# The experts' weights in one host array: three pieces of 2 MB an expert, one 16 KB run a partition, one transfer a piece

## The chip, the cores and the metric

The kernel runs on one core of a Trainium2 chip. The metric is the time of the program on the device in microseconds; lower is better. Three runs of the kernel before took 1817.59, 1819.29 and 1819.63 us, with a median of 1819.29 us.

## The reference

One sequence of 256 tokens with 1024 features goes through three blocks, all in float32. The first two (sparse attention beside Mamba2, a short convolution, each followed by a dense feed-forward) and the attention mixer of the third are not touched. The last part is a mixture of 64 experts in 8 groups. Each token takes two experts; the result is added to the residual, and a last norm follows. For one expert and the tokens `xb` routed to it:

```
def expert_block(args):
    xb, e = args
    return (jax.nn.silu(xb @ w1[e]) * (xb @ w3[e])) @ w2[e]
```

`w1[e]` and `w3[e]` are 1024 x 512 and `w2[e]` is 512 x 1024, so each matrix is 2 MB and one expert has 6 MB. All 64 experts together have 384 MB (402.7 million bytes), and each is read once.

## The kernel before

The dense blocks run first: weights come in chunks of 512 KB, are split into two parts for the float32 products, and are multiplied. `Net.experts` (its lines are in the listing) then goes through the 64 experts in order. For each it needs three *pieces* of 2 MB, which lie in SBUF as tiles of 128 partitions x 4096 floats. There are 11 such tiles, the slots (`NSLOT`), reused in turn: piece `i` goes to slot `i % 11`. Pieces 0 and 1 of an expert hold the first and the second half of the rows of w1 and of w3, and piece 2 holds w2.

`Net.slot` issues the transfers of one piece on SP's queue:

- pieces 0 and 1 are two transfers each (line 1100), one from w1 and one from w3. Each is 1 MB; a partition's share is one run of 8 KB (4 rows of 512 floats) in DRAM.
- piece 2 is one transfer of 2 MB (line 1105). A partition's share is four rows of w2, each a run of 4 KB.
- piece 2 of the last expert alone is four transfers of 512 KB (line 1108), one for each block of 256 output columns; a partition's share of one is four runs of 1 KB. The last product can then begin with the first three blocks.

So an expert takes five issues. The loop over experts goes: every fourth expert, the rows of the tokens of four experts are gathered (`gather`, line 1267); `up` multiplies by w1 and w3 (line 1361); `activate` makes silu(gate) * up (lines 1302 to 1310); `down` multiplies by w2 (line 1420); `spread` and `combine` add the result to the residual in PSUM (lines 1318 and 1329). Then `slot` is called for the three pieces that take the slots just used, `i + 11`.

After the 32nd expert `further` handles experts with more than 32 tokens, one round of 32 at a time. It begins with a branch on the number of such rounds (line 1430) that every engine takes, SP too. Its own loads (tile `mw`) are not among the transfers of the profiled execution. `finish` is the last expert's second product, the last norm and the stores.

The two halves of `slot` before:

```
if w < 2:
    for k, n in enumerate(("w1", "w3")):
        src = self.d[n][e].rearrange("(p j) n -> p (j n)", j=8)
        self.nc.sync.dma_start(t[:, k * 2048:k * 2048 + 2048], src[:, w * 2048:w * 2048 + 2048])
else:
    src = self.d["w2"][e].rearrange("(c p) n -> p c n", p=P)
```

Of the kernel before, what the change touches and what calls it, by code (L numbers as in the profile page):

```python
# [17 lines left out]
PSUM = bass.MemoryType.PSUM  # L18

P = 128  # L20
T = 256
# [61 lines left out]
class Turn:  # L83
    """x^T times the gain of the coming norm, split, [128, 8, 256], and the sums of squares of x. head() begins
    what follows with the first block of tokens."""
# [30 lines left out]
class FinalTurn(Turn):  # L116
    """The turn at the first stack's last norm: x times that norm's gain, and the sums of its squares in ss2."""
# [12 lines left out]
class Routing:  # L130
    """At the last norm: the rows for the experts and the logits."""
# [3 lines left out]
    def head(self):  # L135
        pass
# [45 lines left out]
    def rows(self, b, cols):  # L182
        """columns of a block of tokens, split exactly into three bfloat16 parts: the first of them and the rest."""
        net, nc = self.net, self.net.nc
        c0, c1 = cols
        x = net.x[:, b, c0:c1].rearrange("p (q j) -> p j q", j=8)
        if b:
            rest = self.xT[0][:, c0 // P:c1 // P].rearrange("p k t -> p (k t)")
        else:
            rest = net.xt.tile([P, 512], F32, tag="xg", name="rest", bufs=2)  # L190
        rest = self.rest[b, cols] = rest.rearrange("p (j q) -> p j q", j=8)
        g = net.xg[b][0][:, :, c0 // 8:c1 // 8]
        nc.scalar.activation(g, x, AF.Copy)
        nc.vector.tensor_tensor(rest, x, g, op=ALU.subtract)
# [8 lines left out]
class Net:  # L203
# [44 lines left out]
    def btype(self, srcs, xh, xl, first=None, ps=None):  # L248
        """[128 channels, 2 tiles, 256 tokens] of two chunks of 128 output channels (all of K)."""
        ps = self.acc() if ps is None else ps  # L250
        for m in range(2):
            hi, lo = first[m] if first else self.chunk(srcs[m])
            h3, l3 = (t.rearrange("p (k n) -> p k n", k=KT) for t in (hi, lo))
            for k in range(KT):
                self.mm3(ps[:, m * 256:m * 256 + 256], h3[:, k], l3[:, k], xh[:, k], xl[:, k], k == 0, k == KT - 1)
        return ps.rearrange("p (m t) -> p m t", m=2)

    def rstd_of(self, pool, x, n, width, name):
        """rstd[128, n] from sums of squares [128, n]."""
# [6 lines left out]
    def row_of(self, cols, dst):  # L266
        """dst[128, n*128] = the columns cols[128, n], each as a row along the free axis, on every partition."""
# [7 lines left out]
    def out_chunk(self, src, accs, yh, yl, kt, first):  # L275
        """accs[b][half] += y[kt] @ rows of the chunk."""
# [15 lines left out]
    def out_last(self, srcs, ys, accs, first, turn, scale=None, loaded=None):  # L292
        """The last chunks of a projection onto the residual, one block of tokens after the other and for each some
        columns after the others, so that what follows begins with what is done."""
# [36 lines left out]
    def flip(self, b, ks):  # L331
        """PSUM with x^T of some tiles of features of a block of tokens."""
# [5 lines left out]
    def parts16(self, pool, ps, mask, n, name):  # L338
        """ps[3 n rows, 256], the same n rows three times: row i n + h becomes the i-th bfloat16 part of row h."""
# [115 lines left out]
    def layer0(self, turn):  # L455
        tc, nc, d = self.tc, self.nc, self.d
        with ExitStack() as ctx:
# [51 lines left out]
            with tc.tile_pool(name="dsa", bufs=1) as dp:  # L509
                # ckv, iw, dt (token major) and ik (channel major, twice)  # L510
# [113 lines left out]
    def steps(self, op, dtr, dt, a, eb):  # L624
        """dt = softplus(dtr), a = -dt exp(A_log); eb: minus the running sums of a in each chunk, and what is
        left of chunk 0 after each of its tokens."""
# [25 lines left out]
    def mamba_in(self, xh, xl, rb2, xs, zs, bc, cb, eb):  # L652
# [19 lines left out]
        def cbt(g):  # L672
            """C B^T, transposed: [s, l] of (chunk 0, 0), (chunk 0, 1), (chunk 1, 1)."""
# [12 lines left out]
        def decays(q):  # L686
            """exp of the sums of a from s to l, times C B^T, transposed: [s, head, l]."""
# [17 lines left out]
    def mamba(self, ctx, xs, zs, cb, dt, decays, yah, yal, turn):  # L705
# [4 lines left out]
        # x dt, token major  # L710
# [63 lines left out]
    def log1p_exp_neg_abs(self, pool, out, x, t):  # L774
        """out = log(1 + exp(-|x|)) = 2 atanh(e / (2 + e))."""
# [31 lines left out]
    def ffn(self, turn, w, nxt):  # L807
        """The first 256 hidden channels come token major (they begin with the first block of tokens alone), the others
        channel major. The up branch stays without the norm's factor, which the residual applies."""
# [101 lines left out]
    def angles(self, pool):  # L911
        """cos and sin of position * frequency, [128, 2, 32], with the angle taken to [-pi, pi] first."""
# [23 lines left out]
    def atype(self, srcs, n, xh, xl):  # L936
        """[128 tokens, n] of each block of tokens."""
# [11 lines left out]
    def mixer(self, turn):  # L949
        tc, nc, d = self.tc, self.nc, self.d  # L950
        gates_pool = tc.tile_pool(name="b2", bufs=1)
        with gates_pool as gp:
# [3 lines left out]
            with tc.tile_pool(name="att2", bufs=1) as ap:  # L956
# [20 lines left out]
                # 8 log sigmoid  # L977
# [53 lines left out]
                def bias(ps, b, h):  # L1031
                    """minus 8 times the running sum of log f at s, for every t: what is left of the sum over
                    s < k <= t is the same for all s."""
# [56 lines left out]
    def slot(self, i, t=None):  # L1090
        """DMA of piece i of the experts' weights (of expert 0, then of expert 1, ...): rows 8 p + j of w1 and of w3
        for j < 4, for the other j, w2."""
# [4 lines left out]
        if w < 2:  # L1097
            for k, n in enumerate(("w1", "w3")):
                src = self.d[n][e].rearrange("(p j) n -> p (j n)", j=8)
                self.nc.sync.dma_start(t[:, k * 2048:k * 2048 + 2048], src[:, w * 2048:w * 2048 + 2048])  # L1100
        else:
            src = self.d["w2"][e].rearrange("(c p) n -> p c n", p=P)
            dst = t.rearrange("p (c n) -> p c n", c=4)
            if e < NE - 1:
                self.nc.sync.dma_start(dst, src)  # L1105
            else:
                for c in range(4):
                    self.nc.sync.dma_start(dst[:, c].rearrange("p (k n) -> p k n", k=4), src[:, :, 256 * c:256 * c + 256])  # L1108
# [19 lines left out]
    def open_slots(self, name, ids, now=True):  # L1128
        """slots, from the lowest address to the highest in the order of ids."""
# [9 lines left out]
    def take(self, pool, v, top, name):  # L1139
        """v[128, 2, 8] with the first place of each value of top[128, 2, 8] set to TAKEN."""  # L1140
# [5 lines left out]
    def route(self, rp, lg):  # L1146
        """From the logits of groups and experts: the place of every token within its two experts, from 1 on."""
# [39 lines left out]
    def gates(self, rp):  # L1187
        """The gate of every token at its experts, and the rounds of 32 tokens past the first: expert e has more[e]
        of them, the rounds of all experts in one row."""
# [10 lines left out]
        # the first of the two: the first place of the largest  # L1200
# [57 lines left out]
    def gather(self, dest, sel, n):  # L1258
        """dest[128, 8, n] = rows times the gain, feature 8p + j at [p, j], of the tokens that sel[128, 2, n] picks."""
# [13 lines left out]
    def split_rstd(self, pool, rstd):  # L1273
        """the factors of the last norm, split exactly into three bfloat16 parts."""
# [8 lines left out]
    def factors(self, sel, n):  # L1283
        """[32 c + slot, n experts]: the norm's factor of the token in each slot of sel, four times."""
# [11 lines left out]
    def activate(self, pool, ps, rs):  # L1296
        """ps[32 c + slot, 256]: gate features 256 c + f for c < 2, up features 256 (c - 2) + f after them, both
        without the norm's factor rs.
        Returns silu(gate) * up as [128 f, half, c, slot]."""
# [13 lines left out]
    def spread(self, pool, dg):  # L1313
        """the gates dg[128 tokens, 2, 32 c + slot] as [32 c + slot, 256 tokens]."""
# [8 lines left out]
    def combine(self, y, dT, cs=range(4), last=False, busy=0):  # L1323
        """adds y[32 c + slot, 256] to columns 256 c of the tokens."""
# [9 lines left out]
    def sel(self, e, n):  # L1334
        """sel[128 tokens, 2, 32 slots of expert e, of expert e + 1, ...]: which token each slot takes."""
# [75 lines left out]
    def busy(self, rhs, n, lhs=None):  # L1411
        """n products that nobody reads: the array's clock stays up while the last weights arrive."""
# [5 lines left out]
    def down(self, ps, h, w2, k, c, o=None):  # L1418
        o = k * 1024 + c * 256 if o is None else o
# [3 lines left out]
    def further(self, mp):  # L1423
        """Experts with more than 32 tokens: one round of 32 more at a time."""
# [5 lines left out]
        with tc.If(n > 0), tc.For_i(0, n, 1):  # L1430
# [25 lines left out]
            for j in range(8):  # L1456
                for i in range(2):
                    w = mp.tile([P, 512], F32, tag="mw", name="mw")
                    src = d[("w1", "w3")[i]][bass.ds(r, 1)].rearrange("e (p j) n -> p (e j n)", j=8)
                    nc.sync.dma_start(w, src[:, j * 512:j * 512 + 512])  # L1460
# [5 lines left out]
            for k in range(4):  # L1466
                src = d["w2"][bass.ds(r, 1)].rearrange("e (c p) n -> p (e c) n", p=P)
                for i in range(2):
                    w = mp.tile([P, 512], F32, tag="mw", name="mw")
                    nc.sync.dma_start(w, src[:, k, i * 512:i * 512 + 512])  # L1470
# [9 lines left out]
    def finish(self, mp, h, w2, dg, fn):  # L1480
        """The last expert's second product, a block of 256 columns after the other; self.res[c][token, 256 b:][:256]
        is then the residual sum: its norm, and out."""
# [9 lines left out]
        def down(c0, c1):  # L1492
            ps = self.wk()
            for k in range(4):
                for c in range(c0, c1):
                    self.down(ps, h, w2, k, c, c * 1024 + k * 256)
# [107 lines left out]
def layouts(i):  # L1604
# [63 lines left out]
    d["w1"], d["w3"], d["w2"] = i["w1_2"][0], i["w3_2"][0], i["w2_2"][0]  # L1668
# [17 lines left out]
```

## Time and profile before

| | before |
|---|---|
| median of 3 runs | 1819.29 us (1817.59 to 1819.63) |
| span of the profiled execution, first to last instruction | 1817.2 us |
| TensorE busy (share of the span) | 1536.6 us (85%) |
| VectorE, ScalarE busy | 687.9 us (38%), 525.5 us (29%) |
| mean granted TensorE clock | 0.939 of full speed |
| read from HBM | 542.34 MB |

The span is that of one profiled execution. The page gives no other time for this execution; the median of the runs is 2.1 us above its span. Times in the rows below are microseconds from the start of the span, unless marked ns. "Busy" TensorE includes pipelined matmuls, so it is not TensorE at its peak. The share of the 16 DMA engines can be above 1, since the packets of one engine overlap a little in the record.

### The profile page before, as it was taken

The page shows a single profiled execution, that of the slowest core. Times are in us where ns is not written, and L with a number is a line of the kernel's source. Part 1 is how long each engine was busy: PE and PEld are TensorE (multiplying, and loading weights), DVE is VectorE, ACT ScalarE, POOL GpSimd, SP SyncE. Part 2 cuts the span into 40 slices and gives each one's busy share as a digit, 9 for nine tenths or more (in the row PEclk, how much of TensorE's full clock was granted, in tenths as well). Part 3 has the DMA queues.
Part 4 walks back from the last instruction along what each step waited for, and adds up shares of the span by engine and source line. Part 5 has one row for each costly group of instructions (what it writes and reads, how often), then busy time and mean ns, then how long its engine had stood idle before and what let it go on. Part 6 is the DMA issues. An engine that isn't in the chain of part 4 may idle for free. (4 is left out here: it accounts for less than half of the span.)

```text
span 1817.2 us, 34068 instructions
## 1 busy us (share of the span) xinstructions
PE 1536.6 (85%) x14763; PEld 1136.6 (63%) x14763; DVE 687.9 (38%) x1327; ACT 525.5 (29%) x903; POOL 12.7 (1%) x16
## 2 busy tenths in 40 slices
PE   8999999999999999999886677677676767776676
PEld 7988899989899988798553333333343433433333
DVE  6887755577655567457410111011011101110111
ACT  5585544444544455555200000000000000000001
POOL 0000000000000000000000000000000000000000
PEclk9999999999999999999998988888888998888989
DMA  8344876555555523376999999999999999999997
GB/s 295 102 137 139 287 282 185 186 164 185 194 180 186 187 88 117 109 275 217 382 415 415 416 417 415 416 416 416 416 398 371 416 415 416 416 415 415 416 416 277
DMA packets 112856, 545.64 MB, mean 300 GB/s; under 512 B 10048, under 2 KB 12480, under 8 KB 79936
## 3 DMA queue, kind: packets, MB, share of 16 engines
q1 hardware_dynamic: 112704, 543.43, 77.9%
q8 instruction: 118, 1.93, 0.4%
q14 instruction: 34, 0.28, 0.0%
HBM read 542.34 MB, written 1.05 MB: 299 GB/s over the span
## 5 line engine op out<-in xcount | busy, mean ns | idle before, releaser
L1361 PE MATMUL wk<-w,xe 128*32 128x256 f32 x4096 | 322.2, 410 | 103.0 <-DMA w<-in_w 98.2
L233 DVE TENSOR_TENSOR wlo<-raw,whi 128x1024 fp32r<-128x1024 f32 (+1 forms) x208 | 252.6, 1219 | 152.2 <-ACT whi L232 150.8
L1361 PEld LDWEIGHTS wk<-w,xe 128*32 128x32 f32 x4096 | 146.8, 115 | 249.2 <-DMA w<-in_w 142.3
L232 ACT ACTIVATE whi<-raw 128x1024 fp32r<-128x1024 f32 (+1 forms) x208 | 217.8, 1055 | 251.0 <-PE wk L239 100.2
L1420 PE MATMUL wk<-w,h 128*32 128x256 f32 x2048 | 170.0, 483 | 103.2 <-DMA w<-in_w 87.4
L1310 DVE TENSOR_TENSOR h<-wk,sl 128x128 f32<-128x128 f32 x64 | 18.6, 291 | 526.2 <-ACT sl L1308 526.2
L1420 PEld LDWEIGHTS wk<-w,h 128*32 128x32 f32 x2048 | 83.6, 132 | 164.8 <-issue 117.9
L1302 ACT ACTIVATE a<-wk,rs 128x256 f32<-128x256 f32 x64 | 30.4, 474 | 533.5 <-PE wk L1361 533.5
L238 PE MATMUL wk<-xh,whi 128*128 128x256 f32 x640 | 181.4, 283 | 0.0
L240 PE MATMUL wk<-xh,wlo 128*128 128x256 f32 x640 | 181.1, 283 | 0.0
L239 PE MATMUL wk<-xl,whi 128*128 128x256 f32 x640 | 181.0, 283 | 0.0
L238 PE MATMUL acc<-xh,whi 128*128 128x256 f32 x616 | 177.7, 289 | 1.3 <-ACT whi L232 1.0
L240 PE MATMUL acc<-xh,wlo 128*128 128x256 f32 x616 | 177.3, 288 | 1.3 <-DVE wlo L233 1.3
L239 PE MATMUL acc<-xl,whi 128*128 128x256 f32 x616 | 177.2, 288 | 0.0
L239 PEld LDWEIGHTS wk<-xl,whi 128*128 128x128 f32 x640 | 122.7, 192 | 0.8
L238 PEld LDWEIGHTS wk<-xh,whi 128*128 128x128 f32 x640 | 122.7, 192 | 0.8
L240 PEld LDWEIGHTS wk<-xh,wlo 128*128 128x128 f32 x640 | 122.7, 192 | 0.0
L238 PEld LDWEIGHTS acc<-xh,whi 128*128 128x128 f32 x616 | 119.5, 194 | 4.3 <-issue 1.8
L240 PEld LDWEIGHTS acc<-xh,wlo 128*128 128x128 f32 x616 | 119.5, 194 | 3.2 <-DVE wlo L233 1.7
L239 PEld LDWEIGHTS acc<-xl,whi 128*128 128x128 f32 x616 | 119.6, 194 | 1.4 <-issue 1.3
L1396 DVE COPY y<-wk 128x256 f32<-128x256 f32 x63 | 26.7, 424 | 236.5 <-PE wk L1420 236.5
L1320 ACT COPY dT<-wk 128x256 f32<-128x256 f32 x64 | 23.8, 373 | 283.0 <-PE wk L1318 283.0
(401 smaller groups left out, 2043.7 us busy)
## 6 DMA issues: line engine op xcount, KB each, us to landing
w<-in_w SPq DMA_DIRECT2D x256, 1024.0 KB, 23.1
w<-in_w SPq DMA_DIRECT2D x63, 2048.0 KB, 25.1
raw<-in_l_gu_b SPq DMA_DIRECT2D x80, 512.0 KB, 4.0
raw<-in_l_down SPq DMA_DIRECT2D x44, 512.0 KB, 3.7
raw<-in_l_b SPq DMA_DIRECT2D x28, 512.0 KB, 4.7
raw<-in_l_in SPq DMA_DIRECT2D x24, 512.0 KB, 3.5
raw<-in_l_out SPq DMA_DIRECT2D x20, 512.0 KB, 4.0
w<-in_b_gl SPq DMA_DIRECT2D x16, 512.0 KB, 3.8
```

Of the source, the lines that this page charges most:

```text
L232: nc.scalar.activation(hi[:, :n], raw[:, :n], AF.Copy)
L233: nc.vector.tensor_tensor(lo[:, :n], raw[:, :n], hi[:, :n].bitcast(F32), op=ALU.subtract)
L238: mm(ps, sh, mh, start=start, stop=False, **kw)
L239: mm(ps, sh, ml, start=False, stop=False, **kw)
L240: mm(ps, sl, mh, start=False, stop=stop, **kw)
L1302: nc.scalar.activation(a, ps[:, :256], AF.Copy, scale=rs)
L1310: nc.vector.tensor_tensor(h, p5[:, :, 1], sl, op=ALU.mult)
L1320: nc.scalar.copy(dT, ps[:, :T])
L1361: nc.tensor.matmul(ps[32 * c:32 * c + 32, :256], xe[:, j, e % 4 * 32:e % 4 * 32 + 32], w13[j // 4][:, o:o + 256], start=j == 0, stop=j == ...
L1396: nc.vector.tensor_copy(y, ps[:, :256])
L1420: self.nc.tensor.matmul(ps[32 * c:32 * c + 32, :256], h[:, k % 2, (k // 2) * 32:(k // 2) * 32 + 32], w2[:, o:o + 256], start=k == 0, stop= ...
```

## The change

A new host array `wx` of 64 x 3 x 128 x 4096 floats takes the place of the three arrays w1, w3 and w2. `wx[e, w]` is piece `w` of expert `e` exactly as it lies in SBUF: 128 partitions, each with its 4096 floats (16 KB) in one run. A piece is one transfer of 2 MB, the last piece of all four transfers of 512 KB with one run of 4 KB a partition in each. An expert takes three issues.

In SBUF, pieces 0 and 1 keep their order. In w2's piece the order is now column block, then row block, for all experts (`c * 1024 + k * 256`); before, the last expert alone had this order, and the others `k * 1024 + c * 256`. `down` reads at the other offset; the products and their order are the same. The branch `further` reads from `wx` too. The host's rearrangement lies outside the measured time. Lines that held a docstring or a comment are now blank.

```diff
     def slot(self, i, t=None):
...
         e, w = divmod(i, 3)
-        if w < 2:
-            for k, n in enumerate(("w1", "w3")):
-                src = self.d[n][e].rearrange("(p j) n -> p (j n)", j=8)
-                self.nc.sync.dma_start(t[:, k * 2048:k * 2048 + 2048], src[:, w * 2048:w * 2048 + 2048])
-        else:
-            src = self.d["w2"][e].rearrange("(c p) n -> p c n", p=P)
-            dst = t.rearrange("p (c n) -> p c n", c=4)
-            if e < NE - 1:
-                self.nc.sync.dma_start(dst, src)
-            else:
-                for c in range(4):
-                    self.nc.sync.dma_start(dst[:, c].rearrange("p (k n) -> p k n", k=4), src[:, :, 256 * c:256 * c + 256])
+        parts = 4 if i == 3 * NE - 1 else 1
+        n = 4096 // parts
+        for c in range(parts):
+            self.nc.sync.dma_start(t[:, c * n:c * n + n], self.d["wx"][e, w, :, c * n:c * n + n])
         self.pieces[i] = t
...
-    def down(self, ps, h, w2, k, c, o=None):
-        o = k * 1024 + c * 256 if o is None else o
+    def down(self, ps, h, w2, k, c):
+        o = c * 1024 + k * 256
...
-                    src = d[("w1", "w3")[i]][bass.ds(r, 1)].rearrange("e (p j) n -> p (e j n)", j=8)
-                    nc.sync.dma_start(w, src[:, j * 512:j * 512 + 512])
+                    src = d["wx"][bass.ds(r, 1), j // 4].rearrange("e p n -> p (e n)")
+                    o = i * 2048 + j % 4 * 512
+                    nc.sync.dma_start(w, src[:, o:o + 512])
...
-                src = d["w2"][bass.ds(r, 1)].rearrange("e (c p) n -> p (e c) n", p=P)
+                src = d["wx"][bass.ds(r, 1), 2].rearrange("e p (c k n) -> p (e c) k n", c=4, k=4)
...
-                    nc.sync.dma_start(w, src[:, k, i * 512:i * 512 + 512])
+                    nc.sync.dma_start(w.rearrange("p (c n) -> p c n", c=2), src[:, 2 * i:2 * i + 2, k])
...
-    d["w1"], d["w3"], d["w2"] = i["w1_2"][0], i["w3_2"][0], i["w2_2"][0]
+    wx = d["wx"] = np.empty((NE, 3, P, 4096), f)
+    for w in range(2):
+        for k, n in enumerate(("w1_2", "w3_2")):
+            rows = i[n][0].reshape(NE, P, 8, 512)[:, :, 4 * w:4 * w + 4]
+            wx[:, w, :, 2048 * k:2048 * k + 2048] = rows.reshape(NE, P, 2048)
+    wx[:, 2] = i["w2_2"][0].reshape(NE, 4, P, 4, 256).transpose(0, 2, 3, 1, 4).reshape(NE, P, 4096)
```

## Rows read from the trace of the kernel before

**Rows 1.** The page, DMA in 40 slices, packets by size, instruction queue.
```profile
DMA  8344876555555523376999999999999999999997
GB/s 295 102 137 139 287 282 185 186 164 185 194 180 186 187 88 117 109 275 217 382 415 415 416 417 415 416 416 416 416 398 371 416 415 416 416 415 415 416 416 277
DMA packets 112856, 545.64 MB, mean 300 GB/s; under 512 B 10048, under 2 KB 12480, under 8 KB 79936
...
q8 instruction: 118, 1.93, 0.4%
```

**Rows 2.** Stretches: us, PE, PEld, DVE, ACT, POOL busy (count), PEclk, DMA share, GB/s.
```profile
760.00:810.00 50.00, 50.00 (x393) 45.41 (x393) 27.54 (x42) 31.10 (x52) 0.00 (x0) 1.00 0.67 251
...
872.00:877.00 5.00, 4.79 (x92) 3.18 (x93) 2.67 (x16) 1.00 (x2) 0.00 (x0) 1.00 0.58 176
...
888.00:1346.00 458.00, 332.21 (x4374) 178.00 (x4366) 56.15 (x171) 36.36 (x97) 0.00 (x0) 0.90 1.02 416
1346.00:1359.00 13.00, 8.65 (x102) 4.36 (x106) 0.29 (x1) 0.75 (x2) 0.00 (x0) 0.86 1.01 413
1359.00:1367.60 8.60, 6.48 (x70) 2.61 (x66) 1.02 (x3) 0.37 (x1) 0.00 (x0) 0.81 0.45 185
1367.60:1370.00 2.40, 1.85 (x28) 0.84 (x28) 0.00 (x0) 0.44 (x1) 0.00 (x0) 1.00 0.44 104
1370.00:1786.00 416.00, 291.89 (x3710) 155.04 (x3710) 46.43 (x139) 31.56 (x84) 0.00 (x0) 0.89 1.02 416
1786.00:1803.00 17.00, 14.73 (x154) 8.01 (x155) 1.01 (x3) 1.77 (x5) 0.00 (x0) 1.00 0.87 326
```

**Rows 3.** Waits: engine line, waited for: us in total, times, longest.
```profile
PE wk L1361 <- DMA w<-in_w: 98.2, 82, 3.3
...
SPq L1100 <- DMA w<-in_w: 147.6, 143, 3.5
...
SPq L1430 <- SPq L1430: 20.6, 9, 5.1
```

**Rows 4.** TensorE in order of time, first product of two neighbouring experts (58 of 64 matmuls).
```profile
930.54 3.64 PE L1361 MATMUL wk<-w,xe 128*32 128x256 f32 x58
...
939.83 3.64 PE L1361 MATMUL wk<-w,xe 128*32 128x256 f32 x58
```

**Rows 5.** DMA issues of the experts' weights: count, KB each, median us to landing.
```profile
w<-in_w SPq DMA_DIRECT2D x256, 1024.0 KB, 23.1
w<-in_w SPq DMA_DIRECT2D x63, 2048.0 KB, 25.1
```

**Rows 6.** Stretches in which w1 and w3 alone move (8 KB runs), three of nine.
```profile
929.50:936.50 7.00, 5.68 (x90) 3.21 (x92) 0.39 (x2) 0.75 (x2) 0.00 (x0) 1.00 1.01 414
...
1391.70:1398.70 7.00, 6.13 (x64) 2.84 (x68) 1.02 (x3) 0.37 (x1) 0.00 (x0) 0.76 1.02 421
...
1452.00:1459.00 7.00, 5.92 (x82) 3.11 (x82) 0.95 (x3) 0.37 (x1) 0.00 (x0) 1.00 1.02 421
```

**Rows 7.** Stretches in which w2 alone moves (4 KB runs), three of ten.
```profile
893.20:896.20 3.00, 1.68 (x24) 0.69 (x20) 0.29 (x1) 0.75 (x2) 0.00 (x0) 1.00 1.03 410
909.00:911.50 2.50, 2.50 (x48) 2.24 (x40) 0.69 (x1) 0.00 (x0) 0.00 (x0) 1.00 1.01 405
...
1477.10:1479.80 2.70, 1.93 (x29) 0.92 (x29) 0.00 (x0) 0.47 (x1) 0.00 (x0) 1.00 1.03 411
```

**Rows 8.** SP's issues in order of time, one expert: start, us, count.
```profile
952.11 13.09 SPq L1100 DMA_DIRECT2D w<-in_w  x4
965.29 1.93 SPq L1105 DMA_DIRECT2D w<-in_w  x1
```

**Rows 9.** The end in order of time: last piece, last expert's second product.
```profile
1778.18 17.94 SPq L1108 DMA_DIRECT2D w<-in_w  x4
...
1801.94 4.13 PE L1420 MATMUL wk<-w,h 128*32 128x256 f32 x32 [0.47 <-DVE h L1310]
1802.65 2.93 PEld L1420 LDWEIGHTS wk<-w,h 128*32 128x32 f32 x28 [0.57 <-DMA w<-in_w]
```

More of the change, by code (lines that the diff above doesn't have):

```diff
@@ L1495, in down @@
                 for c in range(c0, c1):
-                    self.down(ps, h, w2, k, c, c * 1024 + k * 256)
+                    self.down(ps, h, w2, k, c)
             nc.vector.tensor_copy(y[32 * c0:32 * c1], ps[32 * c0:32 * c1, :256])
```

## The prediction

> **What bounds the kernel now.** I read the 40 slices first. The kernel has two halves. Up to slice 19 the DMA engines are partly idle; from slice 20 to slice 38 they are at nine tenths or more and move 415 to 417 GB/s, except in slices 29 and 30 [rows 1]. The table by stages shows the first half bound by TensorE: from 760 to 810 us it is busy all of the time while DMA moves 251 GB/s [rows 2]. In the second half TensorE waits 98 us for the experts' weights in its first product alone [rows 3]. Where it doesn't wait, one expert takes it 9.3 us (939.83 less 930.54, [rows 4]); at 416 GB/s an expert's 6.29 MB take 15.1 us. So the transfers set the time there with some 5.8 us an expert to spare on TensorE, and what the change is worth is read from the rate of these transfers.
>
> Three disturbances stand in this half [rows 2]. From 872 to 877 us DMA is at 176 GB/s, because TensorE has not yet freed the first slots. From 1359 to 1367.6 us it is at 185 GB/s and then until 1370 us at 104: SP has come to the branch of line 1430 and waits 20.6 us in nine waits [rows 3], until all that is in flight has landed; the 16 engines don't finish together, so half of them idle. The same shows at the end, 326 GB/s from 1786 to 1803 us.
>
> From 888 us on, then, the transfers run without a pause but for the branch. The bytes of that time are the products of the stretches [rows 2]: 458 x 416 + 13 x 413 + 8.6 x 185 + 2.4 x 104 + 416 x 416 + 17 x 326 = 376.3 MB. Without the last piece (2.1 MB, cost apart below) this is 374.2 / 6.291 = 59.5 experts. The others are loaded before, under TensorE's work.
>
> **What a run costs.** The page counts 112856 packets, of which 79936 are under 8 KB; 32920 are of 8 KB or more [rows 1]. The w1 and w3 transfers are 256 [rows 5] of 128 partitions: 32768 runs of 8 KB. So a run of 8 KB is one packet. While w1 and w3 alone move, the rate is 414 to 421 GB/s in nine stretches, median 420, four of them 421; while w2 alone moves (4 KB runs) it is 405 to 411 in ten short ones, mean 409 [rows 6, 7]. I take 421 and 409: an undisturbed expert then takes 15.09 us, and the 416 of the whole stretch (15.12) leaves room for instruction fetches. Sixteen engines work side by side, so a packet of 8 KB takes 16 x 8192 B / 421 GB/s = 311.3 ns and one of 4 KB 16 x 4096 / 409 = 160.2 ns. The second 4 KB cost 151.1 ns; the fixed part of a packet is 160.2 - 151.1 = 9.1 ns.
>
> **The change part by part.**
>
> *Longer runs.* Each engine handles 8 partitions of a transfer. Before, an expert is 32 packets of 8 KB and 32 of 4 KB on each engine: 32 x 311.3 + 32 x 160.2 = 15.088 us. After, it is 24 of 16 KB. A data packet of 16 KB is not in the rows, so its price is carried on in a line: 311.3 + 2 x 151.1 = 613.5 ns, that is 427 GB/s, and 24 x 613.5 = 14.724 us. The gain is 0.364 us an expert, and over 59.5 experts 21.7 us.
> The price is bounded by the rows themselves. With the lowest w2 rate, 405, and the highest w1 rate, 421, the line gives 610.3 ns, 0.492 us an expert and 29.3 us in all; with 411 and 414 it gives 630.8 ns, 0.096 us and 5.7 us. I take the middle, because the undisturbed stretches repeat 421.
> The Trainium skill ("DMA: Bandwidth & Descriptors", section "Why small descriptors are slow (HBM only)") puts the fixed part at about 3 cycles a packet and says that joining descriptors pays only at 256 B or less. At the 850 MHz that the page gives, 3 cycles are 3.5 ns; by that estimate 40 packets fewer on each engine save 0.14 us an expert, 8.4 us in all. The rows here, with 9.1 ns, say more than twice that.
>
> *The last piece.* Its four transfers have 4 KB runs instead of 1 KB. TensorE waits 0.57 us for it in the second product, after waiting for h at 1801.9 us [rows 9]. However early it lands, no more than that 0.6 us can come back, since h itself waits for the piece before. I count 0.6 us.
>
> *Three issues for five.* SP spends 13.1 + 1.9 us on the five issues of an expert [rows 8], but mostly waits: for a transfer before to land (147.6 us in 143 waits, [rows 3]). With 23 to 25 us from issue to landing [rows 5] and 3.0 us a transfer, about 8 are in flight, 10 MB. Eight of 2 MB would be 16.8 MB, 39 us of work, in 8 of the 11 slots; three stay for TensorE, which after landing needs less than 9.3 us for all three pieces of an expert. So the engines should not run dry, and fewer issues alone gain nothing; the cost is nothing, covered by at least 7 pieces in flight. If that cover went, an idle engine would cost its own time.
>
> *One landing for two halves.* TensorE can't begin with w1 of a piece before w3 has landed. The products of each j go through w1 and w3 in turn, so it waited for w3 after two matmuls anyway. Nothing.
>
> *The branch and the fetches.* SP waits at line 1430 for all that is in flight; it will arrive earlier, with more in flight, and the pause after the last landing stays. Uneven engines and the 118 instruction packets [rows 1] stay as well. No gain is taken there. *The first half.* The first pieces go out beside a busy TensorE [rows 2]: nothing. *The other offset in* `down`: the same reads of SBUF elsewhere: nothing. *The loop in* `further` has no loads in the trace: nothing.
>
> Sum: 1817.2 - 21.7 - 0.6 = 1794.9 us of span; against the runs' median, 2.1 us above the span, 1797.0 us.
>
> **The rivals.**
>
> *The cost isn't per run, or 16 KB are cut to 8 KB.* Then w2 alone gets faster, to w1's rate: 48 x 311.3 = 14.942 us, 0.146 us an expert, 8.7 + 0.6 us in all: 1810.0 us. For it: no data packet over 8 KB is seen, and 421 may be the rate of the memory. Against it: the instruction queue moved 1.93 MB in 118 packets, 16 KB each [rows 1], so the engines do take such packets.
>
> *Run length doesn't matter from 4 KB on.* The difference between 421 and 409 would then lie in short stretches badly cut or in the tiles' order, and the new rate would be the 416 of now: 1818.7 us with the tail. Against it: every one of the ten w2 stretches is below every w1 stretch [rows 6, 7]. The Trainium skill ("DMA: Bandwidth & Descriptors", section "Specifications") gives 512 B as the smallest transfer at line rate; by that rule this is the outcome, and the trace doesn't bear it out as far as 411 against 414 shows.
>
> *Slower: the generator cuts a 16 KB run into packets of 4 KB.* Then every piece costs what w2 costs: 96 x 160.2 = 15.379 us, 0.291 us an expert more, 17.3 us in all, less 0.6: 1836.0 us. It decides from pieces under 6.1 KB (151.1 + 9.1 x 4096/n equals the 157.2 ns that 4 KB cost now on average). For it: 16 KB from this queue is unseen. Against it: 8 KB runs pass whole.
>
> **How the numbers follow.** The line carried on, 0.76; the w1 rate for all, 0.09; no change, 0.06; cut to 4 KB, 0.06; slower by something unseen, such as engines running dry, 0.03. The first two are faster: 0.85; the same, within 0.2% (3.6 us, about what a measurement of this kernel can tell): 0.06; slower 0.09. The time is that of the first, 1797 us. Its bounds are 1819.3 - 29.9 = 1789.4 and 1819.3 - 6.3 = 1813.0 us; these hold the first two cases, and I give 1788 to 1813.
>
> **What would show it.** Right: the page lists packets of 8 KB or more that are fewer by 8320 (191 pieces of 128 runs, 24448, for 32768), the saturated slices read 424 to 428 GB/s, SP issues 195 weight transfers (191 pieces and four parts of the last), with 30 to 40 us to landing, and TensorE still waits for weights. Wrong: slices at 421 (the second case), at 416, or near 409 (cut); or slices that dip while SP waits for TensorE, which would mean that 11 slots are too few for transfers of 2 MB. The pause at the branch should again be some 10 us of half the rate; if it grows, part of the gain goes there.

## The result, and the profile after

| | before | after |
|---|---|---|
| median of the runs | 1818.8 us (4 runs) | 1797.76 us (1796.95 to 1799.92, 4 runs) |
| ratio, 95% interval | | 0.9882 (0.987 to 0.9894) |
| span of the profiled execution | 1817.2 us | 1798.0 us |
| mean granted TensorE clock | 0.939 | 0.930 |

The forecast was 1797.0 us. The time fell by 21.0 us where 22.3 were forecast. Beside further kernels on two other occasions the changed kernel took 1797.46 us (before: 1819.77) and 1797.75 us (before: 1820.31), 22.3 and 22.6 us less.

The page of the changed kernel, with the lines that answer to [rows 1]:

```profile
DMA  7334785555565524266899999999998999999996
GB/s 287 109 130 142 287 286 184 183 164 187 187 188 188 187 73 152 95 249 227 326 426 425 426 426 426 426 424 427 426 424 362 426 426 425 427 426 425 427 425 284
DMA packets 68694, 545.61 MB, mean 303 GB/s; under 512 B 8000, under 2 KB 8384, under 8 KB 44096
...
q8 instruction: 117, 1.92, 0.4%
```

The slices that read 415 to 417 now read 424 to 427. Packets of 8 KB or more are 68694 - 44096 = 24598, against 32920 before: 8322 fewer, where 8320 were expected if a run of 16 KB goes as one packet. It does.

The stretches of the changed kernel (columns as in [rows 2]), cut at its own branch and end:

```profile
900.00:1349.00 449.00, 316.41 (x4336) 177.95 (x4325) 55.19 (x168) 35.93 (x96) 0.00 (x0) 0.88 1.01 426
1349.00:1361.00 12.00, 9.40 (x114) 4.73 (x114) 1.03 (x3) 0.37 (x1) 0.00 (x0) 0.86 0.52 195
1361.00:1363.00 2.00, 0.44 (x2) 0.20 (x2) 0.29 (x1) 0.75 (x2) 0.00 (x0) 1.00 0.79 311
1363.00:1770.00 407.00, 277.98 (x3719) 154.25 (x3720) 46.39 (x139) 31.49 (x83) 0.00 (x0) 0.87 1.01 426
1770.00:1784.00 14.00, 12.49 (x142) 6.63 (x143) 0.72 (x2) 1.49 (x4) 0.00 (x0) 1.00 0.77 317
```

Both long stretches run at 426 GB/s; the pause at the branch is there again, 12 us at 195 GB/s.

Its waits (columns as in [rows 3]), TensorE's first product:

```profile
PE wk L1353 <- DMA w<-in_wx: 113.7, 60, 4.4
```

SP's queue:

```profile
SPq L1100 <- DMA w<-in_wx: 727.2, 160, 6.1
...
SPq L1422 <- SPq L1422: 38.7, 9, 5.4
```

And its issues of the experts' weights (columns as in [rows 5]):

```profile
w<-in_wx SPq DMA_DIRECT2D x191, 2048.0 KB, 39.2
w<-in_wx SPq DMA_DIRECT2D x4, 512.0 KB, 30.1
```

TensorE still waits for weights (113.7 us in its first product, 98.2 before [rows 3]), so the transfers are still the bound. SP's wait at the branch (now line 1422) grew from 20.6 to 38.7 us, since more is in flight, but the pause of the transfers did not grow with it.

The first gather of the experts, before and after, splits the span in two:

```profile
870.31 1.38 PE L1267 MATMUL wk<-sel,xg 128*128 128x32 bf16 x48 [0.48 <-DVE sel L1339]
```

```profile
872.95 1.38 PE L1259 MATMUL wk<-sel,xg 128*128 128x32 bf16 x48 [0.48 <-DVE sel L1331]
```

From it to the end there were 1817.2 - 870.31 = 946.9 us before and 1798.0 - 872.95 = 925.05 us after. The experts' half gained 21.8 us; the first half took 2.6 us longer in this execution (below).

### The profile page after: what moved, and what is told of

Its sections match the earlier page's. It is cut to its first block, busy times and chain, and to the rows that moved or that the text cites. A ratio compares the mean times of both kernels' runs of the same rounds, so it can differ in the third digit from the quotient of the medians.

```text
span 1798.0 us, 33939 instructions
## 1 busy us (share of the span) xinstructions
PE 1507.8 (84%) x14763; PEld 1137.4 (63%) x14763; DVE 688.3 (38%) x1327; ACT 525.5 (29%) x903; POOL 12.7 (1%) x16
## 2 busy tenths in 40 slices
DMA packets 68694, 545.61 MB, mean 303 GB/s; under 512 B 8000, under 2 KB 8384, under 8 KB 44096
## 5 line engine op out<-in xcount | busy, mean ns | idle before, releaser
L1353 PE MATMUL wk<-w,xe 128*32 128x256 f32 x4096 | 286.1, 421 | 119.3 <-DMA w<-in_wx 113.7
## 6 DMA issues: line engine op xcount, KB each, us to landing
w<-in_wx SPq DMA_DIRECT2D x191, 2048.0 KB, 39.2
```

Source lines behind the costliest of these rows:

```text
L1353: nc.tensor.matmul(ps[32 * c:32 * c + 32, :256], xe[:, j, e % 4 * 32:e % 4 * 32 + 32], w13[j // 4][:, o:o + 256], start=j == 0, stop=j == ...
```

## The experiments

All are timed against the kernel before on the same chip. The theory is that each packet has a fixed cost of about 9 ns; the rivals are that fewer and larger issues bring the gain, or the order of a piece in DRAM.

**One piece as two transfers of 1 MB.** The array stays as in the changed kernel.

```diff
-        parts = 4 if i == 3 * NE - 1 else 1
+        parts = 4 if i == 3 * NE - 1 else 2
```

> The changed kernel with each piece issued as two transfers of 1 MB, 8 KB a run (6 issues an expert). Theory (a fixed cost of about 9 ns on every packet): 48 packets of 8 KB on an engine, 48 x 311.3 = 14.94 us an expert against 15.09 before and 14.72 after, so 1810 us, saturated stretches at 421 GB/s. Rival 'fewer and larger issues': six transfers of 1 MB are more than the five of before, so 1819 us or more. Rival 'order in DRAM' (a piece is one stretch of 2 MB): the stretch is still one, so 1798 us.

Measured: 1814.33 us against 1820.05, ratio 0.9964 (0.995 to 0.9978).

**One transfer of 2 MB with two runs of 8 KB.**

```diff
-            self.nc.sync.dma_start(t[:, c * n:c * n + n], self.d["wx"][e, w, :, c * n:c * n + n])
+            self.nc.sync.dma_start(t.rearrange("p (h n) -> p h n", h=2),
+                                   self.d["wr2"][e, w].rearrange("h p n -> p h n"))
...
+    d["wr2"] = np.ascontiguousarray(wx.reshape(NE, 3, P, 2, 2048).transpose(0, 1, 3, 2, 4))
```

The last piece keeps its four transfers here and in the two kernels with shorter runs.

> The changed kernel with the host's array cut so that a partition of a piece has two runs of 8 KB; still one transfer of 2 MB and three issues an expert, the piece still one stretch of DRAM. Theory (fixed cost per packet): the same 48 packets as with two halves, so 1810 us and 421 GB/s. Rival 'fewer and larger issues' and rival 'order in DRAM': both as in the changed kernel, 1798 us and 426 GB/s.

Measured: 1812.05 us, ratio 0.9956 (0.9942 to 0.9969).

**The same with four runs of 4 KB** (`wr4`, 1024 floats a run).

> As the last, with four runs of 4 KB a partition; one transfer of 2 MB a piece. Theory (fixed cost per packet): 96 packets of 160.2 ns on an engine, 15.38 us an expert, 17 us over the kernel before: 1836 us, 409 GB/s. Both rivals: 1798 us.

Measured: 1836.83 us, ratio 1.0089 (1.0074 to 1.0105), slower than the kernel before.

**The same with eight runs of 2 KB** (`wr8`, 512 floats a run).

> The changed kernel with the array cut so that a partition of a piece has eight runs of 2 KB; one transfer of 2 MB, three issues an expert. Theory (a packet costs 9.1 ns and 151.1 ns for each 4 KB): 192 packets of 84.7 ns on an engine, 16.25 us an expert, 69 us over the kernel before: 1889 us, saturated stretches at 387 GB/s. Rivals (issues, order in DRAM): 1798 us. If it is far over 1889, short runs have a cost beyond a fixed one.

Measured: 1892.11 us against 1819.77, ratio 1.0393 (1.0377 to 1.0409).

One stretch of each, from 1450 to 1700 us (columns as in [rows 2]; the last is the rate). Two transfers of 1 MB, 8 KB runs:

```profile
1450.00:1700.00 250.00, 177.41 (x2236) 88.69 (x2228) 28.95 (x83) 17.96 (x48) 0.00 (x0) 0.92 1.01 419
```

One transfer, 8 KB runs:

```profile
1450.00:1700.00 250.00, 166.23 (x2226) 90.86 (x2226) 28.14 (x85) 18.34 (x49) 0.00 (x0) 0.87 1.01 419
```

One transfer, 4 KB runs:

```profile
1450.00:1700.00 250.00, 163.40 (x2184) 89.16 (x2188) 27.46 (x84) 18.03 (x48) 0.00 (x0) 0.88 1.03 408
```

One transfer, 2 KB runs:

```profile
1450.00:1700.00 250.00, 170.01 (x2073) 90.41 (x2076) 26.75 (x81) 17.14 (x46) 0.00 (x0) 0.80 1.04 386
```

The changed kernel, 16 KB runs:

```profile
1450.00:1700.00 250.00, 168.85 (x2260) 91.66 (x2260) 28.49 (x86) 19.09 (x51) 0.00 (x0) 0.86 1.01 426
```

In the last four the number of transfers, the size of a transfer and its 2 MB of DRAM are the same; the length of a run differs, and the rate goes from 386 to 426. The distance in DRAM between a partition's runs differs with it (256 KB, 512 KB and 1 MB for runs of 2, 4 and 8 KB). At 8 KB two layouts were run, this one and the two transfers of 1 MB (16 KB from one partition's run to the next's), and both gave 419, so there the distance does not set the rate; at 2 and 4 KB one layout each was run. The DMA share of 1.01 to 1.04 says that the engines were busy all the time in each. As in the prediction, a packet takes 16 x its bytes / the rate:

| run | rate, GB/s | a packet | 9.2 ns + 75.7 ns for each 2 KB |
|---|---|---|---|
| 2 KB | 386 | 84.9 ns | 84.9 ns |
| 4 KB | 408 | 160.6 ns | 160.6 ns |
| 8 KB | 419 | 312.8 ns | 312.0 ns |
| 16 KB | 426 | 615.4 ns | 614.8 ns |

The line is drawn through the first two rows alone; the other two fall on it within 0.3%. The traces also record how long each single packet took: in this stretch the medians are 88, 164, 313 and 614 ns, and packets of 4 bytes, sixteen for each transfer, took 9 ns. Both rivals fail: they gave 1798 us for 4 KB and for 2 KB runs in one transfer, and the measured times are 39 and 94 us above that.

Between one transfer of 2 MB and two of 1 MB, both with 8 KB runs, lie 2.3 us, with intervals that overlap. Of the 3059 packets that the first has more, 3057 are under 512 B. Two transfers of 1 MB:

```profile
DMA packets 96201, 545.64 MB, mean 301 GB/s; under 512 B 11057, under 2 KB 11441, under 8 KB 47153
```

One transfer of 2 MB:

```profile
DMA packets 93142, 545.61 MB, mean 302 GB/s; under 512 B 8000, under 2 KB 8384, under 8 KB 44096
```

The 3057 more are one for each of the 16 engines and each of the 191 further transfers (3056). At the 9 ns that a packet of 4 bytes took they are 191 x 9 = 1.7 us of an engine, which fits, but the times don't settle it.

**w2 alone, and w1 and w3 alone.** The kernel before with one part of the change each.

The first, w2 alone:

```diff
         else:
-            src = self.d["w2"][e].rearrange("(c p) n -> p c n", p=P)
...
+            parts = 4 if i == 3 * NE - 1 else 1
+            n = 4096 // parts
+            for c in range(parts):
+                self.nc.sync.dma_start(t[:, c * n:c * n + n], self.d["wx"][e, w, :, c * n:c * n + n])
```

The second, w1 and w3 alone:

```diff
         if w < 2:
-            for k, n in enumerate(("w1", "w3")):
-                src = self.d[n][e].rearrange("(p j) n -> p (j n)", j=8)
-                self.nc.sync.dma_start(t[:, k * 2048:k * 2048 + 2048], src[:, w * 2048:w * 2048 + 2048])
+            self.nc.sync.dma_start(t, self.d["wx"][e, w])
```

> The kernel before with w2's piece alone in the new form (one run of 16 KB a partition, the last piece in runs of 4 KB); w1 and w3 as before, five issues an expert. Theory (fixed cost per packet): 32 x 311.3 + 8 x 613.5 = 14.87 us an expert, 0.218 us less, 13.0 + 0.6 us in all: 1805 us. Rival 'fewer and larger issues': the number and size of the transfers are those of before, so 1819 us. Rival 'order in DRAM': a transfer of w2 read one whole stretch of 2 MB before and does so now, w1 and w3 alternate as before, so 1819 us.

Measured: 1807.89 us against 1820.05, ratio 0.9931 (0.9918 to 0.9945): 12.2 us less, where the theory gave 13.6.

> The kernel before with the pieces of w1 and w3 alone in the new form (one transfer of 2 MB, 16 KB a run); w2 as before in runs of 4 KB, the last piece in runs of 1 KB; three issues an expert. Theory (fixed cost per packet): 16 x 613.5 + 32 x 160.2 = 14.94 us an expert, 8.7 us less in all than before, no gain at the last piece: with before at 1820 on this chip, 1811 us; with the 12 us of w2 alone the two parts should add up to the whole change. Rival 'fewer and larger issues' (all the issues that the change saves are saved here): 1798 us.

Measured: 1811.47 us against 1819.77, ratio 0.9959 (0.9945 to 0.9972): 8.3 us less, where the theory gave 8.7.

Their stretches, w2 alone first:

```profile
1450.00:1700.00 250.00, 177.94 (x2258) 94.26 (x2258) 27.77 (x84) 18.71 (x50) 0.00 (x0) 0.89 1.01 421
```

```profile
1450.00:1700.00 250.00, 165.09 (x2256) 92.42 (x2256) 27.31 (x83) 18.04 (x49) 0.00 (x0) 0.89 1.01 420
```

The two parts add up: 12.2 + 8.3 = 20.5 us, against 21.0 to 22.6 for the whole. w2 is a third of the bytes and more than half of the gain, since its packets were the shortest. And w2 alone leaves the number of issues as it was, while w1 and w3 alone save all of them: the gain doesn't follow the issues.

**The branch early, and late.** Where is the pause at the branch paid?

```diff
-            if e == NE // 2 - 1:
+            if e == 1:
```

> The changed kernel with the branch on further rounds after the second expert instead of the 32nd. There TensorE is the bound and the first pause of the transfers lies anyway (no free slot). If all of the disturbed stretch at the branch is lost time (10 us at 165 GB/s and 4 us at 328 of 426, that is 7 us), the kernel comes to 1791 us. If the slowest of the 16 engines sets the time, the fast ones' idle time there is no loss, only the restart of some 2.4 us is, and the unevenness of the engines runs on to the end instead: 1795 to 1798 us, with a longer stretch of half the rate at the end.

Measured: 1800.26 us, ratio 0.9892 (0.9877 to 0.9907); the changed kernel beside it took 1797.46 us, ratio 0.9878 (0.9863 to 0.9893). Neither forecast came: there is no gain, but 2.8 us more by the medians, and the four runs of one (1799.15 to 1800.65) lie above all four of the other (1796.92 to 1798.64). Three stretches of this kernel, at the early branch, at the place of the old one, and at the end:

```profile
900.00:920.00 20.00, 17.22 (x259) 10.10 (x252) 3.08 (x9) 2.24 (x6) 0.00 (x0) 0.97 0.82 332
1340.00:1376.00 36.00, 27.28 (x382) 15.36 (x374) 5.36 (x16) 2.62 (x7) 0.00 (x0) 0.84 1.01 426
1768.00:1784.00 16.00, 13.19 (x147) 7.37 (x148) 0.71 (x2) 1.49 (x4) 0.00 (x0) 1.00 0.59 241
```

The early branch has a pause of its own (332 of 426 GB/s over 20 us, 4.4 us). The 7 us of the old pause did not come back: the last 16 us run at 241 GB/s, as though the half-idle time had moved to the end. That the early place costs nothing of its own, as was expected, was wrong.

> The changed kernel with the branch on further rounds after the 61st expert, when SP has issued all pieces and has nothing more to issue behind it. If the slowest of the 16 engines sets the time, the restart of some 2.4 us goes away and the unevenness (half the rate) is all at the end: 1795 to 1796 us, 2 us under the changed kernel. If the half-idle stretch at the branch was lost time, 7 us go: 1791 us. If TensorE's own stop at the branch (5.8 us with the early branch) can't be made up in three experts, the end comes later: 1798 to 1803 us.

The edit is `e == NE - 4` in the same line. Measured: 1796.15 us against 1820.31, ratio 0.9869 (0.9853 to 0.9886); the changed kernel beside it 1797.75 us, ratio 0.9878 (0.9861 to 0.9894).

> The changed kernel beside it on the same chip: 1797 to 1798 us.

Its stretches at the place of the old branch and at the end:

```profile
1340.00:1400.00 60.00, 38.40 (x544) 21.82 (x544) 6.93 (x21) 4.49 (x12) 0.00 (x0) 0.91 1.01 426
1768.00:1782.00 14.00, 12.85 (x138) 7.13 (x139) 1.14 (x3) 1.33 (x4) 0.00 (x0) 1.00 0.33 135
```

The pause in the middle is gone, and the end runs at 135 GB/s for 14 us (its last 3.5 us move nothing) instead of 317. By the medians it is 1.6 us faster, and its four runs lie below the four of the changed kernel (1793.92 to 1796.92, 1797.38 to 1798.37); the intervals of the ratios overlap, so that this version is faster is likely and not shown. A gain of 7 us did not come.

The traces tell what the pause costs. They list every packet, so one can count how many of 512 B or more are under way at a moment. At the changed kernel's branch 16 are under way until 1350 us, eight from 1352.5 to 1356, and none from 1359 to 1360; with the late branch eight are under way at the end from 1768 to 1776. The DMA share of these two stretches is a half:

```profile
1352.50:1356.00 3.50, 2.51 (x32) 1.32 (x32) 1.03 (x3) 0.37 (x1) 0.00 (x0) 0.91 0.49 208
```

```profile
1768.00:1776.00 8.00, 7.98 (x88) 4.07 (x88) 0.00 (x0) 0.21 (x1) 0.00 (x0) 1.00 0.49 199
```

So half of the engines finish before the others. What the slower half itself loses at the branch, the time with fewer than eight packets under way (each missing one counted as an eighth), is 2.1 to 2.6 us in three profiles of the changed kernel, 2.8 us at the early branch and nothing with the late one. This goes with no gain from the early place and one of some 2 us from the late one, and not with 7 us: the idle time of the engines that finish first is not lost. Of the early branch's 2.8 us it explains some 0.6; where the rest comes from is not shown.

**The first half again.** The changed kernel ran once more beside the others.

> The changed kernel as it is, beside the others on the same chip, for comparison: 21 to 22 us under the kernel before. Its trace also tells whether the 2.6 us that the first half took longer in its first profile (872.95 us to the first gather, 870.31 before) comes back: if it is the order of the transfers, it does; if it is the granted clock of that execution, it need not.

Measured: 1797.46 us. In these rows the number ahead of the DMA share (the third from the end) is the granted clock. The kernel before:

```profile
700.00:750.00 50.00, 49.82 (x315) 40.99 (x314) 30.26 (x87) 26.27 (x75) 0.00 (x0) 0.94 0.35 114
750.00:800.00 50.00, 50.00 (x375) 42.72 (x375) 24.89 (x43) 28.76 (x54) 0.00 (x0) 0.99 0.51 188
```

The changed kernel, first profile:

```profile
700.00:750.00 50.00, 49.81 (x321) 40.95 (x320) 30.91 (x91) 26.13 (x75) 0.00 (x0) 0.97 0.37 117
750.00:800.00 50.00, 50.00 (x354) 42.24 (x353) 23.74 (x42) 28.09 (x53) 0.00 (x0) 0.93 0.48 169
```

The changed kernel, second profile:

```profile
700.00:750.00 50.00, 49.81 (x317) 40.95 (x316) 30.94 (x91) 26.07 (x74) 0.00 (x0) 0.95 0.35 117
750.00:800.00 50.00, 50.00 (x372) 42.71 (x372) 24.35 (x43) 28.99 (x54) 0.00 (x0) 0.98 0.50 185
```

Of the two levels, 1.2 and 2.4 GHz, the lower one was granted for (0.06 + 0.01) x 50 / 0.5 = 7 us of these 100 us before, 10 us in the first profile after and 7 us in the second. The first gather came at 870.31, 872.95 and 871.13 us. In the third profile, beside the late branch, it came at 870.72 us. So most of the 2.6 us belongs to that execution and not to the change. Its clock accounts for part of it: 3 us more at half the clock are some 1.5 us of work; the rest was not traced.

## Why the prediction was right

*The bound.* Right: TensorE still waits for weights, and the saturated rate rose by the same share as the time of the experts' half fell (416 to 426 is 2.4%; 946.9 to 925.05 us is 2.3%).

*The price of a packet of 16 KB.* Predicted 613.5 ns by a line through two rates of the trace before; by the rate of the long stretches it is 615.4 ns, and these hold the instruction fetches too. Predicted rate 427, measured 426. The fixed part was read as 9.1 ns and measured as 9.2. That it came so close is in part luck. The prediction took 421, the highest of its w1 rates, and the long stretch with 8 KB runs alone gave 419. With the 419 and 408 of the long stretches the same line gives 617.2 ns and 20.1 us in place of 21.7; one GB/s in either rate moves the gain by some 2 us. The instruction packets of 16 KB, which the prediction named, showed that such a packet goes, but not its price: 0.4% of 16 engines' 1817 us for 118 packets [rows 1] is some 1 us each, where a data packet of that size took 614 ns. The Trainium skill ("DMA: Bandwidth & Descriptors", section "Why small descriptors are slow (HBM only)") gives about 3 cycles, 3.5 ns at its 850 MHz; by that estimate 8 us would have come back. The runs don't agree with it: packets of 2, 4, 8 and 16 KB all carry 9 ns.

*The 59.5 experts.* Predicted 21.7 + 0.6 us for the experts' half, measured 21.8 in the first profile; the second and third took 924.7 us from the first gather to the end, 22.2 us less than before.

*The last piece.* The wait went as predicted. The end of the changed kernel in order of time:

```profile
1783.13 0.29 DVE L1302 TENSOR_TENSOR h<-wk,sl 128x128 f32<-128x128 f32 x1 [9.96 <-ACT sl L1300]
1783.47 2.84 PEld L1412 LDWEIGHTS wk<-w,h 128*32 128x32 f32 x32 [0.71 <-DVE h L1302]
```

The second product now waits for h alone; the wait for the piece, 0.57 us [rows 9], is gone. No run shows by itself what that brought.

*Issues and slots.* Eight transfers of 2 MB in flight, 39 us, were predicted; 39.2 us were measured, and the engines didn't run dry. That the eight of before would stay eight was assumed; with shorter runs in the same transfers it did not (last section). That fewer issues gain nothing was perhaps 1 us too little: five issues to three take two packets of 4 bytes from each engine and expert, at the 9 ns that the trace records for one 1.1 us over 59.5 experts. The rates that the sum started from already carry that cost, so it is not to be added to the sum as it stands.

*The branch.* The pause stayed, as predicted: 8.6 us at 185 and 2.4 us at 104 GB/s before, 12 us at 195 and 2 us at 311 after. Against the full rate that is 6.6 and 7 us.

*The rivals.* The w1 rate for all is what 8 KB runs gave: 5.7 and 8.0 us less than before, where 9.3 was predicted, since 421 was read too high. Cutting to 4 KB is what the 4 KB runs gave: 16.8 us more, 16.7 predicted. So both prices were near, and only the packets of 16 KB decided between them. No change from 4 KB on fell: 4 KB and 16 KB are 39 us apart. The Trainium skill ("DMA: Bandwidth & Descriptors", section "Specifications") has 512 B as the smallest transfer at line rate; here 2 KB runs still gave 386 GB/s where 16 KB gave 426.

## What to carry to other kernels

When the transfers are the bound, count packets, not only bytes: read the rate in stretches where runs of one length move alone, and two lengths give the fixed part and the price of a byte, from which the rate at a third followed here. With lengths this long the fixed part is a small difference of two rates, so give its error in the forecast. It is worth laying out the weights on the host so that a partition's share of a transfer is one run, and the shortest runs gain the most. A pause that only some of the engines had was not lost time here; what counted was how long the slowest ones stood still.

## What the runs showed of the hardware

- A packet cost 9.2 ns plus 75.7 ns for each 2 KB on one of the 16 engines, from 2 KB to 16 KB; the price of the bytes alone would be 16 x 2048 / 75.7 = 433 GB/s.
- The engines drift apart: at the branch of the changed kernel, some 480 us after the first gather, half of them had finished some 6 us before the last one; with the branch out of the way, at the end, some 10 us. The record doesn't name the engine of a packet, so whether it is the same half each time is open. What makes some engines slower was not tried.
- The same 2 MB transfers took 39.2 us from issue to landing with 16 KB runs, 33.4 with 8 KB, 24.2 with 4 KB and 19.9 with 2 KB. At some 4.9 to 5.4 us a transfer that is about 8, 7, 5 and 4 transfers in flight: with short runs fewer are in flight than with long ones. The DMA share stayed at 1.01 to 1.04, so the engines were not idle for it; its cause was not tried.
